# Filling products booked as two matmuls, and a norm's weights spread by products of 128 rows, at the start of a decoder trunk

## The chip, the cores and the metric

The kernel runs on one core of a Trainium2 chip. Its engines are PE (matrix products, with PEld loading the stationary operand), ACT (activations), DVE (vector work), POOL and SP; SP and POOL issue the DMAs. The metric is the device time of one execution in microseconds (us); lower is better.

## The reference, cut to what matters

Two layers over 256 tokens of width 1024. Each adds a mixer and a feed-forward part to `h`, both behind an RMS norm; a last norm gives the output.

```python
def rmsnorm(x, w):
    xf = x.astype(jnp.float32)
    y = xf * lax.rsqrt(jnp.mean(xf * xf, axis=-1, keepdims=True) + EPS)
    return (y * w.astype(jnp.float32)).astype(x.dtype)
...
    h = x
    for l in range(DEPTH):
        h = h + hybrid_mixer(rmsnorm(h, norm_mix_w[l]), w_in[l], ...)
        h = h + swiglu(rmsnorm(h, norm_ffn_w[l]), w_gate_up[l], w_down[l])
    return rmsnorm(h, final_norm_w)
```

The mixer begins with `u = h @ w_in`; its columns for the values `v` are the first that the kernel computes. All that follows here is the first norm, `rmsnorm(x, norm_mix_w[0])`, and those first products.

## The kernel before

Tokens are handled in two tiles of 128 (t = 0 and 1), the width in two halves of 512. A weight matrix comes in pieces of up to 128 x 1024 by DMA from SP (`raw`, line 309, four buffers). ACT rounds each to its high part `wh` (line 324), DVE subtracts to get the low part `wl` (line 331), and a raw buffer is free again when its `wl` is done. Each product is made of three on PE: high by high (line 340), high by low (341) and low by high (342). There are six pairs of `wh` and `wl`. The first job is `v`, in eight pieces of 128 x 512; the second is a job of 352 columns, in four pieces of 128 x 704.

For the first norm, x lands in `h` in four quarters. ACT squares each with a running sum (line 206), DVE adds the sums of a tile (`ms`, line 221), POOL raises them to the power -1/2 (`rstd`, line 226), and DVE forms `sil` = h times rstd times the norm's weights (line 216). The weights arrive as one row (`wb`, 1 x 1024) and are spread to all 128 partitions by two products with a row of ones (`wps`, line 1347), which stay in PSUM. Then PE transposes `sil` (`tr`, line 382; the identity is in `cst`), ACT copies the result to the high part of `xT` (line 206), and DVE forms its low part (line 213).

The order of all instructions is made ahead of time. `Flow` runs a model of the engines: every step is an `Op` with an engine, a cost in ns and a priority, and whenever an engine is free in the model, the ready step of the lowest priority number goes next in that engine's program. What the model decides is the order; the chip then works each engine's program in order, with semaphores. A cost that is too low makes the model place more steps into a gap than fit there.

`warm_pe` fills PE's gaps at the start. It issues two products of zeros of 384 columns, and then, as long as no real product has been issued, single ones of 64 columns (`idle`, line 1332) with priority 1000, so each goes where nothing else is ready in the model. A float32 product is executed as two passes, so each of these stands in the trace as two pieces. The last 128 columns of `zeros` hold, on partition 0, the ones for the spreading. `w_row` issues the w row on SP between the rows of x and the identity, and `rest_of_consts` issues the other constants (128 x 2048) behind the eight pieces of the first job.

Of the kernel before, what the change touches and what calls it, by code (L numbers as in the profile page):

```python
# [16 lines left out]
P = 128  # L17
# [164 lines left out]
def trunk_kernel(  # L182
# [5 lines left out]
    nc = tc.nc  # L188
# [11 lines left out]
    fl = Flow()  # L200
# [8 lines left out]
    def dve(n, pr, fn):  # L209
        return Op("dve", 1.04 * n + 69, fn, pr)  # L210
# [17 lines left out]
    def pe(cost, pr, fn):  # L228
        return Op("pe", cost, fn, pr)

    def mm_cost(n, fp32=False):
        return n * 4 / 2.4 + 4 if fp32 else max(n / 2.4 + 13.4, 110)
# [65 lines left out]
    def feeder():  # L298
        for i, (src, k, n, ev, job) in enumerate(specs):
            if i == 2:  # L300
                fl.set(first_pieces)
                yield rest_pieces
            yield rawS

            def load():
                raw = new_raw()
                dst, at = raw[:, : k * n].rearrange("p (k n) -> p k n", k=k), 0
                for part in src:
                    nc.sync.dma_start(out=dst[:, :, at : at + part.shape[2]], in_=part)
                    at += part.shape[2]  # L310
                return raw

            raw = yield Op("sp", 450, load, job)
            fl.spawn(splitter(raw, k, n, ev, job, fl.transfer(512 * k * n)))
# [982 lines left out]
    def whole():  # L1297
        norms = [Norm(norm_mix_w[0]), Norm(norm_mix_w[1]), Final(final_norm_w)]
        zeros = new_sx("zeros")
        yield sxS  # L1300
        junk = cp.tile([P, 2], F32, tag="junk", name="junk")

        def fills():
            nc.vector.memset(mhalf, -0.5)
            nc.vector.memset(zeros[:, : 3 * P], 0.0)
            nc.vector.memset(zeros[:1, 3 * P :], 1.0)

        def load(dst, src):
            return Op("sp", 450, lambda: nc.sync.dma_start(out=dst, in_=src), -1)

        def x_half(t, n):
            nsl = slice(n * 512, (n + 1) * 512)
            yield load(h[t][:, nsl], x[0, t * P : (t + 1) * P, nsl])
            fl.spawn(arrived(t, n, fl.transfer(4 * P * 512)))

        def arrived(t, n, ns):
            yield ns
            yield from norms[0].half(t, n, -1)

        def warm():  # L1320
            yield Op("act", 1400, lambda: nc.scalar.activation(out=junk, in_=mhalf, func=AF.Copy), -2)

        def warm_pe():

            yield accS
            box = []

            def emit(n, times):
                if not box:
                    box.append(new_acc("idle"))  # L1330
                for _ in range(times):
                    nc.tensor.matmul(box[0][:, :n], lhsT=zeros[:, :P], rhs=zeros[:, :n], start=True, stop=True)  # L1332

            yield pe(WARM * 1700, -2, lambda: emit(3 * P, WARM))
            while not started[0]:
                yield pe(mm_cost(64, True), 1000, lambda: emit(64, 1))
            fl.release(accS)
            fl.release(sxS)

        def spread_w(n):  # L1340

            yield smS
            nsl = slice(n * 512, (n + 1) * 512)

            def emit():
                ps = new_sm("wps")
                nc.tensor.matmul(ps, lhsT=zeros[:1, 3 * P :], rhs=first_w[:1, nsl], start=True, stop=True)
                return ps

            ps = yield pe(mm_cost(512, True), -1, emit)  # L1350
            fl.set(norms[0].wb[n], ps)

        def w_row():
            yield load(first_w[:1, :], norm_mix_w[0].rearrange("(o d) -> o d", o=1))
            fl.spawn(w_arrived(fl.transfer(4 * D)))

        def w_arrived(ns):
            yield ns
            for n in range(2):
                yield from spread_w(n)  # L1360

        def w_free():
            fl.release(wbS)
            for _ in range(2):
                fl.release(smS)

        yield wbS
        first_w = new_wb()
        norms[0].free = w_free
        yield dve(8, -2, fills)  # L1370
        fl.spawn(warm())
        fl.spawn(warm_pe())
        yield from x_half(0, 0)
        yield from x_half(0, 1)
        yield from w_row()
        yield load(ident, consts[:, K_ID : K_ID + P])
        fl.transfer(4 * P * P)
        fl.spawn(feeder())
        yield first_pieces
        yield from x_half(1, 0)  # L1380
        yield from x_half(1, 1)
        fl.set(rest_pieces)
        fl.spawn(rest_of_consts())
        for l in range(DEPTH):
            yield from layer(l, norms[l], norms[l + 1])

    def rest_of_consts():
        yield 9000.0
        yield Op("sp", 450, lambda: nc.sync.dma_start(out=cst[:, K_ID + P :], in_=consts[:, K_ID + P :]), -1)

    with tc.manual_schedule():
        fl.spawn(whole())
        fl.run()
# [50 lines left out]
```

## Time and profile before

| | us |
|---|---|
| median of 3 runs (lowest, highest) | 1300.35 (1299.91, 1300.78) |
| the profiled execution | 1293.97 |
| its span | 1292.2 |
| PE, DVE, ACT, POOL busy in it | 1282.0, 860.5, 739.6, 34.2 |

The profile is of one execution. A row of the trace names an engine, a line of the kernel, the operation and its tiles (out<-in), the count of instructions merged into it, and what ended the engine's idle time ahead of it, if there was any. Busy times of PE overlap from one product to the next, so the distance of two starts says more than a duration.

### The profile page before, as it was taken

To read this page: it belongs to the slowest core of one execution; us is meant where nothing else is said; L and a number is where in the kernel's file an instruction comes from. 1 tells how busy PE (TensorE), PEld (TensorE's weight loads), DVE (VectorE), ACT (ScalarE), POOL (GpSimd) and SP (SyncE) were. 2 spreads that over 40 slices of the span, in tenths; PEclk is the share of its full clock that TensorE was granted. 3 is DMA by queue.
4 is the path that set the end of the run, shared out by engine and by line. 5 is a ranking of instruction groups with operands and counts; after the bars stand their busy time and mean duration, and the time that the engine had idled before them with its cause. 6 is when DMAs were issued, how large, how long until landed. Compare 5 with 4: busy or idle time off the path is not lost.

```text
span 1292.2 us, 17009 instructions
## 1 busy us (share of the span) xinstructions
PE 1282.0 (99%) x6346; PEld 1078.7 (83%) x6346; DVE 860.5 (67%) x1163; ACT 739.6 (57%) x1086; POOL 34.2 (3%) x56
## 2 busy tenths in 40 slices
PE   9999999999999999999999999999999999999997
PEld 7888888888888888888888988888888888788886
DVE  5875788878576665554478658878875756655544
ACT  5765676886365454444367556867955634544432
POOL 1000000000010000000010000000000100000000
PEclk9999999999999999999999999999999999999999
DMA  7757565555465556665566565656555664766551
GB/s 225 230 164 223 163 183 164 177 195 196 147 226 198 166 192 197 183 194 189 162 190 197 165 199 161 187 181 181 196 168 179 199 209 131 233 190 189 188 188 57
DMA packets 129013, 237.67 MB, mean 184 GB/s; under 512 B 7817, under 2 KB 59905, under 8 KB 128802
## 3 DMA queue, kind: packets, MB, share of 16 engines
q1 hardware_dynamic: 127458, 232.16, 57.9%
q0 software_dynamic: 1472, 4.42, 1.2%
q8 instruction: 50, 0.82, 0.3%
q14 instruction: 33, 0.27, 0.1%
HBM read 235.43 MB, written 1.11 MB: 183 GB/s over the span
## 4 chain that ended last, share of the span: by engine, by line
PE 94%; issue 2%; DMA 1%; ACT 1%; DVE 1%; POOL 0%; POOLq 0%; SPq 0%; DVEq 0%; ACTq 0%
PE acc L340 22%; PE acc L342 22%; PE acc L341 22%; PE acc L521 10%; PE acc L522 6%; PE tr L382 3%; PE yps L1060 2%; PE acc L524 1%; DMA raw<-in_w_gate_up_dram 1%; PE idle L1332 1%; PE tr L954 1%; PE sm L819 1%; DVE wl L331 1%; PE ips L1047 0%; ACT wh L324 0%
## 5 line engine op out<-in xcount | busy, mean ns | idle before, releaser
L331 DVE TENSOR_TENSOR wl<-raw,wh 128x1024 fp32r<-128x1024 f32 (+2 forms) x432 | 514.4, 1195 | 306.4 <-ACT wh L324 304.1
L324 ACT ACTIVATE wh<-raw 128x1024 fp32r<-128x1024 f32 (+2 forms) x432 | 443.6, 1035 | 354.7 <-PE acc L342 275.8
L340 PE MATMUL acc<-wh,xT 128*128 128x512 f32 (+1 forms) x896 | 348.3, 389 | 0.0
L341 PE MATMUL acc<-wl,xT 128*128 128x512 f32 (+1 forms) x896 | 342.7, 383 | 0.2 <-DVE wl L331 0.2
L342 PE MATMUL acc<-wh,xT 128*128 128x512 f32 (+1 forms) x896 | 342.8, 383 | 0.0
L521 PE MATMUL acc<-xT,wh 128*128 128x512 f32 x560 | 203.6, 401 | 0.0
L342 PEld LDWEIGHTS acc<-wh,xT 128*128 128x128 f32 x896 | 168.2, 188 | 31.9
L341 PEld LDWEIGHTS acc<-wl,xT 128*128 128x128 f32 x896 | 168.4, 188 | 31.2 <-DVE wl L331 1.1
L340 PEld LDWEIGHTS acc<-wh,xT 128*128 128x128 f32 x896 | 168.3, 188 | 30.2 <-issue 0.9
L522 PE MATMUL acc<-xT,wl 128*128 128x256 f32 x640 | 167.0, 281 | 0.0
L522 PEld LDWEIGHTS acc<-xT,wl 128*128 128x128 f32 x640 | 120.8, 189 | 6.9
L521 PEld LDWEIGHTS acc<-xT,wh 128*128 128x128 f32 x560 | 105.4, 188 | 21.3
L340 PE MATMUL acc<-wh,A 128*128 128x512 f32 x192 | 76.7, 399 | 0.0
L216 DVE SCALAR_TENSOR_TENSOR cb<-ca,cv,cb 128x255 f32<-128x255 f32 (+1 forms) x144 | 68.4, 479 | 10.9 <-ACT cb L206 9.8
L342 PE MATMUL acc<-wh,A 128*128 128x512 f32 x192 | 74.8, 390 | 0.0
L341 PE MATMUL acc<-wl,A 128*128 128x512 f32 x192 | 74.8, 389 | 0.0
L340 PE MATMUL acc<-wh,Y 128*128 128x512 f32 x176 | 70.7, 402 | 0.0
L342 PE MATMUL acc<-wh,Y 128*128 128x512 f32 x176 | 68.7, 390 | 0.0
L341 PE MATMUL acc<-wl,Y 128*128 128x512 f32 x176 | 68.5, 389 | 0.0
L340 PE MATMUL acc<-wh,C 128*128 128x512 f32 x128 | 50.6, 395 | 0.0
L342 PE MATMUL acc<-wh,C 128*128 128x512 f32 x128 | 49.9, 390 | 0.0
L341 PE MATMUL acc<-wl,C 128*128 128x512 f32 x128 | 49.8, 389 | 0.0
(140 smaller groups left out, 1301.3 us busy)
## 6 DMA issues: line engine op xcount, KB each, us to landing
raw<-in_w_in_dram SPq DMA_DIRECT2D x188, 512.0 KB, 4.3
raw<-in_w_gate_up_dram SPq DMA_DIRECT2D x80, 512.0 KB, 3.8
raw<-in_w_down_dram SPq DMA_DIRECT2D x44, 512.0 KB, 3.2
raw<-in_ret_out_dram SPq DMA_DIRECT2D x32, 512.0 KB, 3.6
raw<-in_ssd_out_dram SPq DMA_DIRECT2D x32, 512.0 KB, 3.3
raw<-in_w_in_dram SPq DMA_DIRECT2D x24, 352.0 KB, 3.3
seg<-acs SPq DMA_DIRECT2D x16, 512.0 KB, 5.6
raw<-in_w_o_dram SPq DMA_DIRECT2D x16, 512.0 KB, 3.3
```

Source lines behind the costliest of these rows:

```text
L216: return Op("dve", 1.04 * n + 130, lambda: nc.vector.scalar_tensor_tensor(out=out, in0=in0, scalar=scalar, in1=in1, op0=op0, op1=op1), pr)
L324: nc.scalar.activation(out=wh[:, :m], in_=raw[:, :m], func=AF.Copy)
L331: nc.vector.tensor_tensor(out=wl[:, :m], in0=raw[:, :m], in1=wh[:, :m].bitcast(F32), op=ALU.subtract)
L340: nc.tensor.matmul(ps, lhsT=lh, rhs=rh, start=first, stop=False)
L341: nc.tensor.matmul(ps, lhsT=lh, rhs=rl, start=False, stop=False)
L342: nc.tensor.matmul(ps, lhsT=ll, rhs=rh, start=False, stop=last)
L382: nc.tensor.transpose(out=ps[:, j * P : (j + 1) * P], in_=src[:, j * P : (j + 1) * P], identity=ident)
L521: nc.tensor.matmul(a, lhsT=wh[:, k % 4, fsl], rhs=x[:, k % 4, :, :], start=k == 0, stop=False)
L522: nc.tensor.matmul(a[:, :SEQ], lhsT=wl[:, k % 4, fsl], rhs=xh[:, k % 4, :], start=False, stop=False)
L524: nc.tensor.matmul(a, lhsT=wh[:, k % 4, fsl], rhs=x[:, k % 4, :, :], start=False, stop=True)
L819: nc.tensor.matmul(ps[:, :SEQ], lhsT=k[:, b, :P], rhs=q[:, b, :], start=b == 0, stop=b == 1)
L1060: nc.tensor.matmul(ps[:, i * HD : (i + 1) * HD], lhsT=sg[:, i, :], rhs=xdt[:, i * HD : (i + 1) * HD], start=True, stop=True)
```

## The change

Three edits at the start, in `whole`. A filling product of 64 columns is booked in the model at twice its former cost. The two spreading products take all 128 rows of `zeros` and of `first_w` in place of row 0; for that `zeros` is filled with zeros over all 512 columns, and `first_w` is filled with zeros by POOL. The w row's DMA waits for that fill (`cleared`), and `w_row` runs beside the issue of the identity and no longer ahead of it.

```diff
             nc.vector.memset(mhalf, -0.5)
-            nc.vector.memset(zeros[:, : 3 * P], 0.0)
+            nc.vector.memset(zeros, 0.0)
             nc.vector.memset(zeros[:1, 3 * P :], 1.0)
...
             while not started[0]:
-                yield pe(mm_cost(64, True), 1000, lambda: emit(64, 1))
+                yield pe(2 * mm_cost(64, True), 1000, lambda: emit(64, 1))
...
-                nc.tensor.matmul(ps, lhsT=zeros[:1, 3 * P :], rhs=first_w[:1, nsl], start=True, stop=True)
+                nc.tensor.matmul(ps, lhsT=zeros[:, 3 * P :], rhs=first_w[:, nsl], start=True, stop=True)
...
         def w_row():
+            yield cleared
             yield load(first_w[:1, :], norm_mix_w[0].rearrange("(o d) -> o d", o=1))
...
         yield dve(8, -2, fills)
+        cleared = Event()
+
+        def clear():
+            yield Op("pool", 1000, lambda: nc.gpsimd.memset(first_w, 0.0), -2)
+            fl.set(cleared)
+
+        fl.spawn(clear())
         fl.spawn(warm())
         fl.spawn(warm_pe())
         yield from x_half(0, 0)
         yield from x_half(0, 1)
-        yield from w_row()
+        fl.spawn(w_row())
         yield load(ident, consts[:, K_ID : K_ID + P])
```

On PE, from the first instruction to the first products of the job (`acc`), the fillings between the steps of the norm change their number:

```order
 L1332 MATMUL idle<-zeros 128x384 x2
 L1332 MATMUL idle<-zeros 128x64 x2
 L1347 MATMUL wps<-wb,zeros 128x512 x2
-L1332 MATMUL idle<-zeros 128x64 x7
+L1332 MATMUL idle<-zeros 128x64 x3
 L382 MATMUL tr<-cst,sil 128x128 x4
-L1332 MATMUL idle<-zeros 128x64 x2
+L1332 MATMUL idle<-zeros 128x64
 L382 MATMUL tr<-cst,sil 128x128 x4
-L1332 MATMUL idle<-zeros 128x64 x12
+L1332 MATMUL idle<-zeros 128x64 x6
 L340 MATMUL acc<-wh,xT 128x512
```

Eleven of the 64-column fillings are gone: four ahead of the first transposes, one between them and the second, six ahead of the first real products. The steps of the norm and the products keep their order.

On SP, at the start, the identity (`cst`, 128 x 128) and the w row (`wb`) change places:

```order
 L1309 DMA h_81<-in_x_dram 128x512 x2
+L1309 DMA cst<-consts_dram 128x128
 L1309 DMA wb<-in_norm_mix_w_dram 1x1024
-L1309 DMA cst<-consts_dram 128x128
 L309 DMA raw<-in_w_in_dram 128x512 x2
 L1309 DMA h_82<-in_x_dram 128x512 x2
 L309 DMA raw<-in_w_in_dram 128x512 x6
```

The w row now waits for POOL's fill, and behind it stand the first two weight pieces, the rows of x of the second tile and the other six pieces of the first job. On POOL that fill stands ahead of everything else that the kernel itself asks for. ACT keeps its order, and so does DVE.

## Rows read from the trace of the kernel before

**Rows 1.** The page: busy time, share of the span and instructions of each engine.

```profile
PE 1282.0 (99%) x6346; PEld 1078.7 (83%) x6346; DVE 860.5 (67%) x1163; ACT 739.6 (57%) x1086; POOL 34.2 (3%) x56
```

**Rows 2.** The waits of PE from 20 us to the end: engine, line and tile that waited, what it waited for, us in total, times, longest.

```profile
PE tr L382 <- DVE sil L213: 0.9, 2, 0.5
PE tr L382 <- DVE sil L216: 0.5, 2, 0.3
PE yps L1060 <- ACT seg L1028: 0.4, 1, 0.4
```

**Rows 3.** The timeline of PE, up to the first products of the second job (352 columns): start and duration in us, line, tiles, count.

```profile
4.81 1.98 PE L1347 MATMUL wps<-wb,zeros 1*128 1x512 f32 x4
6.72 2.12 PE L1332 MATMUL idle<-zeros 128*128 128x64 f32 x14
8.63 1.06 PE L382 MATMUL tr<-cst,sil 128*128 128x128 f32 x4
9.49 0.95 PE L1332 MATMUL idle<-zeros 128*128 128x64 f32 x4
10.23 1.06 PE L382 MATMUL tr<-cst,sil 128*128 128x128 f32 x4
11.09 2.94 PE L1332 MATMUL idle<-zeros 128*128 128x64 f32 x24
13.84 0.48 PE L340 MATMUL acc<-wh,xT 128*128 128x512 f32 x1
...
15.48 1.05 PE L382 MATMUL tr<-cst,sil 128*128 128x128 f32 x8
16.28 0.47 PE L340 MATMUL acc<-wh,xT 128*128 128x512 f32 x1
...
19.30 0.49 PE L341 MATMUL acc<-wl,xT 128*128 128x512 f32 x1 [0.23 <-DVE wl L331]
...
27.00 0.32 PE L341 MATMUL acc<-wl,xT 128*128 128x352 f32 x1
```

**Rows 4.** The timeline of ACT: squares of x (sil<-h), copies of the transposes (xT<-tr), and the high part of the first 704-column piece.

```profile
7.71 0.63 ACT L206 ACTIVATE sil<-h 128x512 f32<-128x512 f32 x1 [0.40 <-DMA h<-in_x_dram]
...
9.73 0.60 ACT L206 ACTIVATE xT<-tr 128x512 fp32r<-128x512 f32 x1 [1.29 <-PE tr L382]
10.22 0.62 ACT L206 ACTIVATE sil<-h 128x512 f32<-128x512 f32 x1
...
11.33 0.60 ACT L206 ACTIVATE xT<-tr 128x512 fp32r<-128x512 f32 x1 [0.39 <-PE tr L382]
...
24.95 0.79 ACT L324 ACTIVATE wh<-raw 128x704 fp32r<-128x704 f32 x1 [2.86 <-DMA raw<-in_w_in_dram]
```

**Rows 5.** The timeline of DVE: the fill of zeros, the normed rows, the low halves of xT and of the weight pieces.

```profile
0.93 0.38 DVE L1305 MEMSET zeros<- 128x384 f32 x1
...
6.03 1.54 DVE L216 SCALAR_TENSOR_TENSOR sil<-h,rstd,wps 128x512 f32<-128x512 f32 x2 [0.95 <-PE wps L1347]
...
10.36 0.69 DVE L213 TENSOR_TENSOR xT<-tr,xT 128x512 fp32r<-128x512 f32 x1 [1.59 <-ACT xT L206]
...
11.96 0.69 DVE L213 TENSOR_TENSOR xT<-tr,xT 128x512 fp32r<-128x512 f32 x1 [0.78 <-ACT xT L206]
12.57 1.40 DVE L216 SCALAR_TENSOR_TENSOR sil<-h,rstd,wps 128x512 f32<-128x512 f32 x2
13.88 1.29 DVE L331 TENSOR_TENSOR wl<-raw,wh 128x512 fp32r<-128x512 f32 x2
...
25.77 0.89 DVE L331 TENSOR_TENSOR wl<-raw,wh 128x704 fp32r<-128x704 f32 x1 [2.96 <-ACT wh L324]
```

**Rows 6.** Busy time of each engine by stretch: the stretch in us, its length, busy us and instructions of each engine, the granted clock of PE as a share of full speed, the DMA share, GB/s.

```profile
7.50:8.00 0.50, 0.50 (x7) 0.50 (x6) 0.50 (x2) 0.28 (x1) 0.00 (x0) 0.99 0.75 279
8.00:8.50 0.50, 0.50 (x5) 0.50 (x5) 0.50 (x2) 0.44 (x2) 0.00 (x0) 0.50 1.00 381
...
11.00:11.50 0.50, 0.50 (x5) 0.50 (x4) 0.18 (x2) 0.17 (x1) 0.24 (x1) 0.60 0.13 45
...
12.00:14.00 2.00, 2.00 (x20) 2.00 (x19) 2.00 (x4) 1.48 (x3) 2.00 (x4) 1.00 0.14 31
```

**Rows 7.** The timeline of POOL: the last of four one-column fills that stand ahead of the kernel's own work, and the power of the first tile's norm.

```profile
0.33 0.12 POOL L1430 MEMSET const-uint8-127<- 128x1 uint8 x1
5.16 0.55 POOL L226 TENSOR_TENSOR rstd<-ms,mhalf 128x1 f32<-128x1 f32 x1 [4.71 <-DVE ms L221]
```

**Rows 8.** The timeline of SP's queue: when it issued which DMA.

```profile
0.74 0.87 SPq L1309 DMA_DIRECT2D h<-in_x_dram  x2
1.66 0.33 SPq L1309 DMA_DIRECT2D wb<-in_norm_mix_w_dram  x1
2.03 0.35 SPq L1309 DMA_DIRECT2D cst<-consts_dram  x1
...
3.37 0.91 SPq L1309 DMA_DIRECT2D h<-in_x_dram  x2
...
15.58 0.42 SPq L1389 DMA_DIRECT2D cst<-consts_dram  x1
```

**Rows 9.** Time from issue to landing: first of the four quarters of x, then of the two blocks of constants (the identity is the lowest, the megabyte the highest).

```profile
DMA to landing us min/median/max: 2.7/3.6/5.0
DMA to landing us min/median/max: 3.2/5.4/7.5
```

## The prediction

> **What bounds the kernel now.** I read the page first: PE is busy for 1282.0 us, 99% of the span [rows 1]. The waits of PE from 20 us to the end then show what is left to gain after the start: 1.8 us in five waits [rows 2]. So after 20 us PE sets the time, and what moves its work by a microsecond at 20 us moves the end by a microsecond, unless some transfer does not move along. The whole change lies ahead of 20 us, so I read that stretch engine by engine.
>
> PE looks full there, but most of it is filling [rows 3]. Real products begin only at 13.84. What stands before them is the first norm: the products that spread its weights (wps) at 4.81, the normed rows (sil) on DVE from 6.03, four transposes at 8.63 and four at 10.23, their copies (xT) on ACT at 9.73 and 11.33 [rows 4], and the same for the second 128 tokens, whose eight transposes start at 15.48. The reader should see three things. The first sil was finished at about 6.8 (two in 1.54 us from 6.03 [rows 5]), but its transposes start at 8.63: 14 filling pieces from 6.72 on stand ahead of them. The 24 pieces from 11.09 to 13.84 hold back products whose first operands were there by 11.05 (10.36 plus 0.69, the low half of xT [rows 5]). [...] The four transposes at 8.63 take 0.86 us to the next row, the eight at 15.48 take 0.80: 0.215 against 0.10 each. [...]
>
> Each filling is two pieces. At full clock 24 pieces take 2.75 us [rows 3], 0.115 each, 0.23 a filling; the planner before books 0.11. That is why its fillings overrun, and the new price of 0.22 is about right.
>
> **The change, part by part.**
>
> *Larger zero fill.* DVE's row is 0.38 us for 384 columns [rows 5], 1.0 ns each; 128 more cost 0.13 us. PE is busy from its first filling on, so wps moves from 4.81 to 4.94. It is on the path, but has cover: see the point on the seven fillings.
>
> *POOL's fill, and the w row behind it.* No row shows a POOL fill of 1024 columns. Below: 0.12 us, its one-column fill [rows 7], if width cost nothing. Nearest: DVE's rate, 1.0 us. Above: three times that, 3.0. I take 1.0, because both engines' small fills are of one size (0.12 here). POOL starts when all engines do, about 0.74, SP's first issue [rows 8], so the fill ends near 1.75. SP now issues the identity at 1.66 and the w row at 2.03, and waits for the fill ahead of the latter: at 1.0 it does not wait. All that is queued behind on SP (two weight pieces, the second tokens' rows of x, six pieces) would slip by any such wait, at 3.0 us by 1.7.
>
> *The w row is 0.37 us later.* It was there by 4.81, at most 3.15 after its issue; the identity, issued in the slot it gets now, took 3.2 [rows 9]. So it lands by about 5.2, and wps starts between 4.94 and 5.2. Rows 128 deep cost no more: a transpose does 128 columns in 0.10, so 512 take 0.40, and a wps piece takes 0.48 (four from 4.81 to 6.72). The first sil followed 1.22 behind wps (6.03 less 4.81); it then starts at 6.16 to 6.45 and ends at 6.9 to 7.2.
>
> *Seven fillings become three.* wps and its tail take 1.91 (6.72 less 4.81), so fillings start at 6.85 to 7.1 and six pieces of 0.115 end at 7.5 to 7.8. The transposes start there, not at 8.63. At full clock they take 0.40, and with the 0.24 from the next row to ACT's copy (9.73 less 9.49) xT could start at 8.2 to 8.4. Now ACT is late instead: its square of the second tokens starts at 7.71, because their rows of x land then, and ends after 0.63, and the read of its sum follows [rows 4]. So the copy goes from 9.73 to about 8.5, 1.25 sooner. The next square needs x's last quarter: the longest landing is 5.0 us [rows 9], from an issue near 3.83 [rows 8], so 8.85; it starts at 8.95 in place of 10.22. The second copy follows 0.7 later, at 9.7 in place of 11.33, since its transposes (one filling, 0.23, behind the first ones) are done by 9.0.
>
> On DVE the low half of that copy goes from 11.96 to 10.3, the second tokens' sil from 12.57 to 11.05, and the split low halves (wl) queued behind it from 13.88 to about 12.4: 1.45 sooner. If the clock fell as before, transposes at 0.215 and fillings at 0.185 (four from 9.49 to 10.23) would put the first copy at 8.95, the second at 10.2 and wl at 12.8: 1.1 sooner.
>
> *Twelve fillings become six.* They end near 10.3, the six products of some 1.5 us (13.84 to 15.48, less one filling) near 11.8, and the transposes of the second tokens wait for DVE (11.05 plus two of 0.7) and end near 12.9, in place of 16.28. DVE then runs its four steps of some 0.6 to the last low half of the first job back to back from 13.7: the product that waited for that one moves from 19.30 to 16.3. PE is **3.0 us** ahead here.
>
> *What is late next.* PE cannot keep that. SP issues the big block of constants at 15.58, behind two pieces that waited for the wl of 13.88; it moves by 1.45 only. The first 704-column piece lies behind that megabyte, which takes 7.5 us to landing [rows 9]; ACT waited 2.86 us for it, until 24.95 [rows 4], and DVE's low half of it ended at 25.77 plus 0.89, 26.66 [rows 5]. PE took it at 27.00 [rows 3], 0.3 later. So it is ready 1.45 sooner, at 25.2, where PE would want it at 24.0: a new wait of 1.2 us. The gain is 0.3 and 1.45, less some 0.15 because the pieces meet POOL's small transfers longer: **1.6 us**. The pieces after it are issued as buffers come free and move along.
>
> **The sum.** The profiled execution took 1293.97 us; less 1.6 gives 1292.4. The runs' median is 1300.35, 6.4 above the profiled one; the start is the same work in both, so I take the difference over: **1298.75**.
>
> [...] In the stretch from 8.0 on PE did eight transposes and fillings, and the clock rose after it [rows 3, 6]. [...]
>
> **The rivals.**
>
> *Full gain.* The piece behind the constants comes sooner than I think, because the DMA share was 0.14 at 12 to 14 us [rows 6] and there is room. Then PE keeps 2.75 to 3.0: 1297.5. Against it: 2.86 us of waiting for exactly that transfer.
>
> *The clock falls on real products.* PE now waits near 11.8 and for four wl between 13 and 16.3. At half clock a group of three products takes 1.4 in place of 0.7. A stretch as long as from 8.0 to 11.4 costs 1.7, of which 1.2 is hidden in the new wait: gain 1.1, 1299.2. Two such stretches cost 3.4, and the time is 1300.95.
>
> *POOL's fill is slow, and SP waits.* This one ends on the other side. Each microsecond over 1.3 in the fill goes to SP, to x's rows and to all pieces behind. At 3.0 us nothing is left of the gain; at 6.0 the start is 3.0 later than now: 1303.4. For it: SP works in order, and POOL takes 0.55 for one column of the power at 5.16 [rows 7]. Against: its plain fill of one column takes 0.12.
>
> *The fillings hide nothing.* x's landings hold ACT at 7.71 anyway, and the w row or POOL's first power comes late; 0.3 to 0.9 is left: 1299.8.
>
> **How the numbers follow.** Forecast 0.56 (1298.3 to 1299.2); full gain 0.14; clock 0.08; slow fill 0.07, most of it between no gain and 2 us lost; fillings hide nothing 0.15. The range is 1297.3 to 1300.6: it takes in full gain, one slow stretch and the last case, and leaves out the slow fill, two slow stretches and the tails. A measurement of this kernel can tell about 0.2%, 2.6 us, from no change. Faster than 1297.75 needs nearly the full gain: 0.11. Slower than 1302.95 is the far end of the slow fill, or several slow stretches: 0.04. Between: 0.85.
>
> **What would show it.** POOL's fill of wb near 1.0 us, and no gap on SP ahead of the w row. Six pieces ahead of the first transposes, which start near 7.6 at a granted clock of 1.00. ACT's first copy at 8.5, DVE's third low half near 12.4, the product that waited at 19.30 near 16.3; and then, as the test of the size, a wait of PE near 24 to 25 us for the first 704-column piece. If PE runs through there, the gain is 2.7 or more; if the fill lasts over 3 us, the forecast's sign is wrong.

## The result, and the profile after

The change takes 1291.86 us, median of 4 runs (1291.36 to 1292.69), against 1300.13 for the kernel before in the same comparison: a ratio of 0.9937, interval 0.992 to 0.9954. That is 8.3 us, five times the 1.6 that was forecast, and below the range. The profiled executions tell another story: 1293.97 before and 1291.82 after, 2.15 apart, close to the forecast. So two things have to be explained: the start as the profiles show it, and 6 us that the profiled execution of the kernel before does not have and its other runs do. One execution of all that follow, of e11, took 1836.11 us at a mean granted clock of 0.658 and is left out of every figure below.

First the profile after, in the views that answer to those of before. The timeline of PE, to be read beside [rows 3]:

```profile
4.96 2.71 PE L1347 MATMUL wps<-wb,zeros 128*128 128x512 f32 x4
7.50 0.78 PE L1332 MATMUL idle<-zeros 128*128 128x64 f32 x6
8.12 0.61 PE L382 MATMUL tr<-cst,sil 128*128 128x128 f32 x4
8.56 0.33 PE L1332 MATMUL idle<-zeros 128*128 128x64 f32 x2
8.73 0.61 PE L382 MATMUL tr<-cst,sil 128*128 128x128 f32 x4
9.17 1.45 PE L1332 MATMUL idle<-zeros 128*128 128x64 f32 x12
10.43 0.48 PE L340 MATMUL acc<-wh,xT 128*128 128x512 f32 x1
...
12.08 1.25 PE L382 MATMUL tr<-cst,sil 128*128 128x128 f32 x8
13.08 0.48 PE L340 MATMUL acc<-wh,xT 128*128 128x512 f32 x1
...
16.21 0.50 PE L341 MATMUL acc<-wl,xT 128*128 128x512 f32 x1 [0.23 <-DVE wl L331]
...
24.38 0.42 PE L340 MATMUL acc<-wh,xT 128*128 128x352 f32 x1 [0.47 <-ACT wh L324]
25.31 0.43 PE L341 MATMUL acc<-wl,xT 128*128 128x352 f32 x1 [0.50 <-DVE wl L331]
```

Real products start at 10.43 in place of 13.84, and the product that waited for the last low half of the first job runs at 16.21 in place of 19.30. At 24.38 and 25.31 PE waits for the first 704-column piece, as it did not before. ACT and DVE, beside [rows 4, 5]:

```profile
8.84 0.58 ACT L206 ACTIVATE xT<-tr 128x512 fp32r<-128x512 f32 x1
...
9.93 0.58 ACT L206 ACTIVATE xT<-tr 128x512 fp32r<-128x512 f32 x1
...
23.54 0.79 ACT L324 ACTIVATE wh<-raw 128x704 fp32r<-128x704 f32 x1 [4.02 <-DMA raw<-in_w_in_dram]
```

```profile
0.95 0.48 DVE L1305 MEMSET zeros<- 128x512 f32 x1
...
6.92 1.54 DVE L216 SCALAR_TENSOR_TENSOR sil<-h,rstd,wps 128x512 f32<-128x512 f32 x2 [1.81 <-PE wps L1347]
...
11.15 1.40 DVE L216 SCALAR_TENSOR_TENSOR sil<-h,rstd,wps 128x512 f32<-128x512 f32 x2
12.47 1.29 DVE L331 TENSOR_TENSOR wl<-raw,wh 128x512 fp32r<-128x512 f32 x2
```

The new fill on POOL, and SP's issues, beside [rows 7, 8]:

```profile
0.74 0.95 POOL L1375 MEMSET wb<- 128x1024 f32 x1 [0.29 <-POOLq L1438]
```

```profile
2.13 0.33 SPq L1309 DMA_DIRECT2D wb<-in_norm_mix_w_dram  x1
...
14.16 0.42 SPq L1397 DMA_DIRECT2D cst<-consts_dram  x1
```

The fill ends at 1.69 and SP issues the w row without a wait. The one thing that looks worse than forecast is the first sil, at 6.92: the four spreading pieces start 0.96, 0.73 and 0.43 apart, so the clock rose only while they ran.

### The profile page after: what moved, and what is told of

The parts are those of the page before. It is cut to its first block, busy times and chain, and to the rows that moved or that the text cites. A ratio compares the mean times of both kernels' runs of the same rounds, so it can differ in the third digit from the quotient of the medians.

```text
span 1290.1 us, 16966 instructions
## 1 busy us (share of the span) xinstructions
PE 1279.6 (99%) x6324; PEld 1075.5 (83%) x6324; DVE 860.5 (67%) x1163; ACT 739.4 (57%) x1086; POOL 35.1 (3%) x57
## 4 chain that ended last, share of the span: by engine, by line
PE 87%; DVE 4%; ACT 3%; issue 3%; DMA 3%; POOL 0%; SPq 0%; POOLq 0%; DVEq 0%; ACTq 0%
PE acc L340 21%; PE acc L342 21%; PE acc L341 21%; PE acc L521 9%; PE acc L522 5%; PE tr L382 2%; PE yps L1060 2%; DVE wl L331 2%; DMA raw<-in_w_in_dram 1%; PE acc L524 1%; ACT wh L324 1%; ACT seg L1028 1%; PE sm L819 1%; DMA seg<-acs 1%; PE tr L954 0%
```

## The experiments

The kernel before ran 78 times beside the experiments: 50 runs lie at 1299.0 or above (the late group below), 19 at 1295.5 or below (the early group), 9 between. Its time is therefore two groups with a few runs in the middle, and a kernel is best read by where its runs lie, not by its median alone. The late share differs, 18 of the 35 runs beside e1 to e4 and 32 of the 43 beside the others, so the ratios of those two parts of the table can't be set against each other. The table counts all fillings of a kernel, with the one behind the first six products.

| kernel | spreading rows | fillings of 64 columns | runs: lowest, median, highest | ratio to before (interval) |
|---|---|---|---|---|
| e1, before again | 1 | 24 | 1294.1, 1300.5, 1300.9 | 1.0018 (0.9999 to 1.0036) |
| e2, rows only | 128 | 24 | 1292.3, 1293.2, 1295.4 | 0.9976 (0.9961 to 0.9991) |
| e3, price only | 1 | 13 | 1291.8, 1294.7, 1296.0 | 0.9976 (0.9960 to 0.9993) |
| e4, the change with one row | 1 | 13 | 1291.6, 1293.2, 1296.1 | 0.9968 (0.9951 to 0.9984) |
| e5, the change again | 128 | 13 | 1291.7, 1292.7, 1294.9 | 0.9950 (0.9935 to 0.9966) |
| e6, before, no fillings | 1 | 0 | 1292.4, 1293.1, 1293.8 | 0.9956 (0.9938 to 0.9974) |
| e7, before, wide fillings | 1 | 13 of 256 | 1291.7, 1294.8, 1297.4 | 0.9967 (0.9951 to 0.9983) |
| e8, the change, constants later | 128 | 13 | 1291.3, 1292.4, 1294.2 | 0.9949 (0.9929 to 0.9969) |
| e9, the change, no fillings | 128 | 0 | 1291.4, 1292.8, 1295.9 | 0.9956 (0.9941 to 0.9971) |
| e10, before, half price | 1 | 47 | 1306.8, 1310.1, 1310.9 | 1.0081 (1.0057 to 1.0104) |
| e11, e2 with one row | 1 | 24 | 1293.5, 1297.2, 1300.5 | 0.9984 (0.9967 to 1.0001) |

**e1: the kernel before, once more**, unchanged.

> The unchanged kernel again, for the 6.4 us between its profiled execution (1293.97) and its other runs (1300.1). Theory clock (the one-row spreading products leave the clock low, and for longer in most executions than in the profiled one): runs near 1300 with a mean granted clock of about 0.990 to 0.994, and a profile near 1300 shows 0.50 well beyond 11.4 us. Theory elsewhere (the 6.4 us lie in some later part of the kernel): a clock of 0.997 as in the first profile, and rows that differ only after 20 us.

This time the profiled execution was one of the late group: 1299.67, span 1297.9. Its PE timeline:

```profile
4.96 3.78 PE L1347 MATMUL wps<-wb,zeros 1*128 1x512 f32 x4
8.67 3.25 PE L1332 MATMUL idle<-zeros 128*128 128x64 f32 x14
11.71 1.06 PE L382 MATMUL tr<-cst,sil 128*128 128x128 f32 x4
12.56 0.95 PE L1332 MATMUL idle<-zeros 128*128 128x64 f32 x4
13.31 1.06 PE L382 MATMUL tr<-cst,sil 128*128 128x128 f32 x4
14.16 5.22 PE L1332 MATMUL idle<-zeros 128*128 128x64 f32 x24
19.14 0.77 PE L340 MATMUL acc<-wh,xT 128*128 128x512 f32 x1
...
22.16 1.68 PE L382 MATMUL tr<-cst,sil 128*128 128x128 f32 x8
23.60 0.48 PE L340 MATMUL acc<-wh,xT 128*128 128x512 f32 x1
```

Read the distances: 14 filling pieces in 3.04 us and 24 in 4.98, 0.21 each, where the 24 of the first profile, most of them at a granted clock of 1.00 [rows 6], took 0.115 [rows 3]. Everything up to 23 us went at half clock: the products from 19.72 to 21.85 stand 0.43 apart, where those from 14.15 on in the first profile stand 0.23 apart, and the eight transposes from 22.16 on take 1.44 us, between the 1.70 of that pace (0.85 for four) and the 0.80 of the first profile [rows 3], which puts the rise at about 23.4. Real products began at 19.14, not 13.84, and those behind the second tokens' transposes at 23.60, not 16.28: 7.3 us late, of which 5.7 reached the end (1297.9 against 1292.2). The mean clock of 0.998 that I had expected lower does not show it: the view by stretches reads 1.00 in all of 2 to 29 us of this execution, with the pieces 0.21 apart. So in this execution the 6 us lie in the start and are a matter of the clock. The first profile of before was an execution in which the clock had risen at about 4.6 (PE's weight loads take 0.33 us at 4.30, 0.23 at 4.51 and 0.18 at 5.34) and was low again only from 8.0 to about 11.4 (0.50, and 0.60 at 11.0 to 11.5 [rows 6]). The other runs have no rows, but their mean clocks fit: 46 of the 50 late runs read 0.999 and the other four 0.998, as the profiled execution of e1 does, while 14 of the 19 early ones read 0.997, as the first profile of before does, and five 0.998.

**e2, e3, e4: each edit alone.**

```diff
# e2, against the change
-                yield pe(2 * mm_cost(64, True), 1000, lambda: emit(64, 1))
+                yield pe(mm_cost(64, True), 1000, lambda: emit(64, 1))
# e3, against the kernel before
-                yield pe(mm_cost(64, True), 1000, lambda: emit(64, 1))
+                yield pe(2 * mm_cost(64, True), 1000, lambda: emit(64, 1))
# e4, against the change
-                nc.tensor.matmul(ps, lhsT=zeros[:, 3 * P :], rhs=first_w[:, nsl], start=True, stop=True)
+                nc.tensor.matmul(ps, lhsT=zeros[:1, 3 * P :], rhs=first_w[:1, nsl], start=True, stop=True)
```

> The change without the new price of a filling, so with 128-row spreading products, 23 fillings in place of 12, and the w row behind POOL's fill. Theory clock: 1292.5 to 1294, most of the gain, and a clock of 0.998 or 0.999 in all runs. Theory filling (the fillings' overrun carries the gain): 1298 to 1300. Theory queue (the changed order on SP carries it): as for clock, to be told apart by the run with one row.

> The kernel before with the new price of a filling alone: one-row spreading products, 12 fillings. Theory clock: 1297 to 1300, a clock below 0.997 in its runs, a gain of 0 to 3 us. Theory filling: about 1292. Theory queue: 1298.5, the 1.6 us of the prediction.

> The change with one-row spreading products; the order on every engine, POOL's fill and the place of the w row are those of the change. Theory clock: 1297 to 1300, as with the price alone, because only the rows count. Theories filling and queue: 1291.9, as the change.

All three lie at 1293.2 to 1294.7, and no run of any is above 1296.1. That contradicts each theory as I had put it. The clock theory expected the price alone to leave most runs near 1300; the filling theory expected the rows alone to. Either edit by itself removes the late group, and by the medians the two do not add (6.5 us and 5.1 alone, 7.6 together in e5). So I formed another: a loop. At half clock the fillings take nearly twice as long (0.21 us a piece against 0.115); by the theory they do not bring the clock up, products of the job (the real products) do, and these stand behind the fillings; fewer fillings shorten the loop, spreading products of 128 rows ahead of it keep PE out of it. This is too narrow in one point: in the first profile of before the clock rose at about 11.4 [rows 6], ahead of the first real product at 13.84 [rows 3], and e7 and e11 show the same.

One pair of profiles shows what the rows alone do. e4 and e8 (below) have the same order on PE up to the real products, and in both the clock rose at about 5.0, just as the spreading began: the four spreading pieces take 1.91 us in e4 (5.07 to 6.98) and 1.86 in e8 (4.96 to 6.82), against 3.71 in e1 (4.96 to 8.67). Stretches of 3 us; the column behind the busy times is the granted clock. First e4, with one-row products:

```profile
5.00:8.00 3.00, 3.00 (x14) 1.68 (x14) 1.73 (x4) 1.39 (x3) 0.55 (x1) 1.00 0.97 309
8.00:11.00 3.00, 3.00 (x19) 3.00 (x17) 2.65 (x6) 3.00 (x8) 0.98 (x2) 0.57 0.78 268
11.00:14.00 3.00, 3.00 (x10) 2.52 (x10) 2.42 (x4) 0.76 (x2) 2.39 (x5) 0.50 0.30 50
14.00:17.00 3.00, 3.00 (x17) 2.68 (x17) 0.86 (x2) 1.49 (x3) 0.00 (x0) 0.80 0.88 110
```

Then e8, with 128-row products:

```profile
5.00:8.00 3.00, 3.00 (x17) 2.04 (x17) 1.72 (x3) 1.14 (x2) 0.55 (x1) 1.00 1.00 318
8.00:11.00 3.00, 3.00 (x24) 2.70 (x23) 2.25 (x5) 2.91 (x9) 0.64 (x2) 1.00 0.80 279
11.00:14.00 3.00, 2.48 (x16) 2.03 (x15) 3.00 (x6) 2.37 (x6) 2.74 (x5) 1.00 0.22 45
```

PE is busy for all of 5 to 11 us in both. After one-row products the clock fell at about 8.4 and stayed low until 15.2 (an estimate from the 0.57 of 8 to 11 and the 0.80 of 14 to 17, with the 0.50 and 1.00 that other stretches read); after 128-row products it stayed at 1.00, and the products from 10.07 to 11.00 stand 0.23 apart. The runs agree: eight of the twelve of e4 read a mean clock of 0.996 or 0.997, while all thirteen of the change (with e5) read 0.998 or 0.999. But these eight are the fast ones of e4, at 1291.6 to 1293.7. Its other four, at 1295.2 to 1296.1, read 0.999, as the late runs of the kernel before do.

**e5: the change again**, unchanged.

> The change once more, for how far its executions spread and for a profile in which the clock rises at another moment. Theory loop (at half clock the fillings take twice as long and do not raise the clock, so the real products, which do, come late; 128-row spreading products extend the dense start, so the clock has risen by 11 us in every execution): 1291 to 1293 in all runs, none above 1294. Theory luck (four runs that happened to start well): some runs at 1294 to 1300.

No run is in the late group. Three of nine lie above 1293, and one of them, at 1294.85, is over the bound of 1294. In its profile the spreading pieces take 2.88 us, from 5.31 to 8.19, and in the first profile of the change 2.54, from 4.96 to 7.50. Both lie between the 1.86 of e8 and the 3.71 of e1, so the clock rose during the spreading, by these distances at about 7.5 and 6.5.

**e6, e7: no fillings, and wide ones, in the kernel before.**

```diff
# e6
-            while not started[0]:
-                yield pe(mm_cost(64, True), 1000, lambda: emit(64, 1))
# e7
-                yield pe(mm_cost(64, True), 1000, lambda: emit(64, 1))
+                yield pe(mm_cost(128, True), 1000, lambda: emit(256, 1))
```

> The kernel before, with one-row spreading products, without any 64-column filling; PE idles in their place. Theory loop: no run at 1300; the real products start at 12 to 14 us at either clock, and the time is 1291.5 to 1296, as with the new price alone. Theory guard (the fillings keep the clock up, or bring it up): more runs at 1300 or above, since nothing is left between the one-row products and the real ones but transposes.

> The kernel before with fillings of 256 columns, booked at half of what they take, so that they overrun by about as much time as those of 64 columns did: 13 in place of 24, one-row spreading products. If the width of a filling decides whether it raises the clock (theory loop), the clock rises during the fillings, and the runs lie at 1292.5 to 1296 with none at 1300. If fillings only take time, whatever their width, the runs spread from 1294 to 1301 as before, most at 1300.

Without any filling the kernel before takes 1293.1 with a spread of 1.4 us: the fillings did not guard the clock, they were the delay. In its profile the clock stayed low until about 12 (the products up to 11.66 stand 0.43 to 0.49 apart, from 12.07 on 0.23), and yet the real products began at 9.72, sooner than the 12 to 14 that I had expected:

```profile
7.92 2.03 PE L382 MATMUL tr<-cst,sil 128*128 128x128 f32 x8
9.72 0.79 PE L340 MATMUL acc<-wh,xT 128*128 128x512 f32 x1
```

The wide ones of e7 overrun at least as much (3.57 us ahead of the first transposes, where e1 has 3.04), and yet no run is above 1297.4. Six of the twelve are above the 1296 that I had set, though, at 1296.2 to 1297.4. The PE timeline of one of these:

```profile
8.78 3.78 PE L1332 MATMUL idle<-zeros 128*128 128x256 f32 x8
12.35 1.06 PE L382 MATMUL tr<-cst,sil 128*128 128x128 f32 x4
13.20 0.97 PE L1332 MATMUL idle<-zeros 128*128 128x256 f32 x2
14.01 0.60 PE L382 MATMUL tr<-cst,sil 128*128 128x128 f32 x4
14.45 2.76 PE L1332 MATMUL idle<-zeros 128*128 128x256 f32 x12
16.86 0.58 PE L340 MATMUL acc<-wh,xT 128*128 128x512 f32 x1
```

Four transposes take 0.85 us at 12.35 and 0.44 at 14.01: the clock rose between them, three microseconds ahead of the first real product. With narrow fillings, in e1, it had not. Transposes stood ahead of this rise too, so the profile alone does not show that the width did it.

**e10: twice the fillings in the kernel before.**

```diff
-                yield pe(mm_cost(64, True), 1000, lambda: emit(64, 1))
+                yield pe(mm_cost(64, True) / 2, 1000, lambda: emit(64, 1))
```

> The kernel before with a filling booked at half its former price: 47 fillings where 24 stood, one-row spreading products. Theory loop: at half clock 46 more pieces of 0.213 us stand ahead of the real products, and the clock waits for those: most runs 9 to 10 us later, at 1308 to 1311. Where the clock was up early, 0.115 a piece: 1298 to 1300. If the 1300 state does not come from the fillings, most runs stay at 1300 to 1302.

All six runs are at 1306.8 to 1310.9, 9.7 us behind the kernel before at the median. Four lie where the loop puts them; the other two, at 1306.8 and 1307.0, do not reach the 1298 to 1300 that I had given for an early rise. The profile is of one of these two: the clock was up early (the spreading pieces take 1.90 us, from 5.20 to 7.10), but fell at about 7.9 (0.98 at 5 to 8, 0.50 at 8 to 11). Its PE timeline and its stretches (granted clock behind the busy times):

```profile
15.34 10.77 PE L1332 MATMUL idle<-zeros 128*128 128x64 f32 x50
25.87 0.77 PE L340 MATMUL acc<-wh,xT 128*128 128x512 f32 x1
```

```profile
17.00:20.00 3.00, 3.00 (x16) 3.00 (x15) 2.42 (x4) 0.74 (x2) 1.04 (x2) 0.50 0.38 33
20.00:23.00 3.00, 3.00 (x16) 3.00 (x15) 0.00 (x0) 0.00 (x0) 0.00 (x0) 0.50 0.80 247
23.00:26.00 3.00, 3.00 (x16) 3.00 (x15) 0.00 (x0) 0.00 (x0) 0.00 (x0) 0.50 0.68 270
```

For ten microseconds PE is busy without a gap, with nothing but 64-column fillings, at half clock. The clock rose at about 28.35 (0.61 at 26 to 29), 2.5 us after the first real product. This is the loop in one view.

**e11: e2 with one-row products.** The edit is that of e4, made in e2.

> The run with the rows alone (e2: 128 rows, old price, 23 fillings, POOL's fill, the w row behind the identity), with one-row products in place of 128-row ones; the order is that of e2 on every engine. Theory loop: most runs at 1298 to 1301, since the rows were all that e2 had against the slow state. If the order on SP or the two more fillings ahead of the spreading did it: 1292.5 to 1295.5, as e2.

Of eleven runs five are at 1300.0 or above, where e2 has none above 1295.4; that is fewer than the most that the loop gave. Three lie near 1297, three at 1293.5 to 1294.0, and the median is 1297.2. The order is that of e2 on every engine, so at the old price the rows alone are worth 4.0 us at the median. What is left of e2's gain, the 3.1 us from 1300.3 to 1297.2, is not clear of the spread (the interval of the ratio ends at 1.0001), so a smaller part for the order on SP or the fillings ahead of the spreading is not excluded. At the new price (e4 against e5) the rows are worth 0.5 at the median, and the four runs above 1295 that e4 has are missing in e5.

**e8, e9: what is left.**

```diff
# e8, against the change
-        yield 9000.0
+        yield 20000.0
# e9, against the change
-            while not started[0]:
-                yield pe(2 * mm_cost(64, True), 1000, lambda: emit(64, 1))
```

> The change with the megabyte of constants issued later, behind the four pieces of 128 x 704 and three more. It removes the wait of PE at 24 to 25 us for the first of those pieces (0.65 and 0.75 us in the profile of the change). If that wait was what took back a part of the gain, the first product of the second job starts 1.3 us sooner and the time is 0.5 to 1.3 us below the change; if the next pieces are late by as much, the same as the change.

> The change without any 64-column filling. Theory loop: the clock rises during or right behind the 128-row spreading products as in the change, and what is left of the overrun goes too: 1291 to 1292.5, a median 0 to 0.7 us below the change. Theory guard (twelve fillings keep the clock up until the real products): the clock falls in some executions, up to 1294.

Neither differs from the change by more than its runs spread, and neither forecast of a gain came true. In e8 the wait at 24 us is gone, and another one stands a job later:

```profile
23.74 0.32 PE L340 MATMUL acc<-wh,xT 128*128 128x352 f32 x1
...
38.32 0.50 PE L340 MATMUL acc<-wh,xT 128*128 128x512 f32 x1 [1.12 <-ACT D L206]
```

The first product of the second job starts 0.64 us sooner than in the profile of the change (23.74 against 24.38), where 1.3 was forecast, the second 1.41 sooner; at 38.32 only 0.4 of the lead is left (38.74 in the change).

In e9 the median, 1292.8, is no better than that of e5, and five of twelve runs lie at 1293.75 to 1295.91, where e5 has one of nine above 1293.5. Two of these five read a mean clock of 0.997, as the first profile of before, in which it fell. That is what the theory of the guard gave, so with 128-row products the twelve fillings may do some good; the runs don't settle it. No version was found that beats the change.

## Why the prediction was wrong

**The step that failed** is the sum: "the start is the same work in both, so I take the difference over". The profiled execution lay 6.4 us below a median whose three runs spread by 0.9. I took that as an offset common to both kernels. It was the very cost that the change removes: in the late executions of the kernel before the clock stays low until the real products, and the profiled one had escaped. In e1, the one late execution with a profile, the clock was low until about 23.4 us, and PE was 7.3 us late, of which 5.7 reached the end. That the other late runs are like it is argued from their times and mean clocks. What half clock costs was in the rows: fillings at 0.185 a piece there against 0.115 [rows 3, 6]. Without the offset the sum says 1292.4, and 1291.86 was measured.

**Luck.** That the two profiles differ by 2.15, close to the 1.6, is in part luck: they are of executions with different clocks. Before, the clock was up from 4.6 to 8.0 and low until about 11.4 [rows 6]; after, it was low until 6.5 and up from there. In e8, with the same order on PE and a rise at about 5.0, the real products began at 9.75 in place of 10.43.

**The larger zero fill** cost 0.10 (0.48 less 0.38), and PE's first filling moved from 1.36 to 1.49, by the 0.13 forecast. That wps started at 4.96 for 4.94 does not show it: in e1 it starts at 4.96 too, without the larger fill. **POOL's fill** took 0.95 for 1.0, with luck: I took DVE's rate for POOL's because their small fills are of one size, but DVE's fill of two columns takes 0.06 and POOL's of one 0.12. SP did not wait, the w row went out at 2.13 for 2.03 and landed in time in this profile; in that of e5 wps started at 5.31, 0.1 over my bound.

**Seven fillings to three.** They end at 8.12 for 7.5 to 7.8, because the clock rose only during the spreading, which took 2.54 in place of 1.91. ACT's copies came at 8.84 and 9.93 for 8.5 and 9.7, the second sil at 11.15 for 11.05, wl at 12.47 for 12.4. **Twelve to six.** They end at 10.43 for 10.3; the second tokens' transposes at 13.08 for 12.9; the product that waited at 16.21 for 16.3. **What is late next** was right in place and size: constants issued at 14.16 for 14.13, the piece's high part at 23.54 for 23.5, and PE took the low half at 25.31 for 25.2. The gain there is 27.00 less 25.31, 1.69 for 1.6; the 0.15 that I took off for POOL's small transfers has no row in any run. The profiles' spans end 2.1 apart, 0.4 more than that; behind 26 us PE waits 0.7 us in place of 1.8 [rows 2], which may be where it comes from.

**The rivals.** Full gain did not come, for the reason given: PE's lead of 3.09 us at 16.21 was 1.69 at 25.31. The slow fill did not happen. That the fillings hide nothing is refuted by the profile after (real products at 10.43 for 13.84), by e6 and by e10. A fall of the clock on real products did not come in the profile after: the granted clock is 1.00 throughout, and from 16.55 to 22.71 the products stand 0.22 to 0.24 apart. Three products at half clock take 1.28 us (19.72 to 21.00 in e1) against 0.70 (14.15 to 14.85 in the first profile of before), not 1.4. The clock rival looked at the wrong kernel: I asked whether the change would let the clock fall on real products, and not whether the clock was low on those of the kernel before in the runs that set its median, as it was in e1 until about 23.4. And the fall to 0.50 at 8.0 in the first profile [rows 6], behind one-row products and narrow fillings [rows 3], I took for a fact of that one execution and gave no price in the others.

## What to carry to other kernels

If a profiled execution lies outside the spread of the other runs, the profile is of another case: find what differs before taking its rows as a price for the median. A filling product that overruns its price delays the work behind it, at half clock nearly twice as much (0.21 us a piece against 0.115). None was shown to be worth its place here: without any, the kernel before took 1293.1 and the change 1292.8, no more than with them. A filling booked at what it takes at half clock, about 0.42 us, was not tried. After such an edit, read the clock from the distance of like products, and several runs instead of one.

## What the runs showed of the hardware that I had not expected

Products with one row of operands did not hold the clock, though PE was busy for as long: with them the clock fell at about 8.4 and was 0.50 at 11 to 14 (e4), with 128 rows it was 1.00 from 5 to 14 (e8). Width seems to count too: fifty 64-column pieces back to back left it at 0.50 for ten microseconds (e10), while with 256-column ones in the place of narrow ones no run of twelve was late (e7, highest 1297.4).

Transposes may bring the clock up. In e11 nothing but eight transposes and narrow fillings stood between the one-row products and the rise; PE's timeline:

```profile
11.85 1.06 PE L382 MATMUL tr<-cst,sil 128*128 128x128 f32 x4
12.70 0.95 PE L1332 MATMUL idle<-zeros 128*128 128x64 f32 x4
13.45 1.05 PE L382 MATMUL tr<-cst,sil 128*128 128x128 f32 x4
14.30 2.82 PE L1332 MATMUL idle<-zeros 128*128 128x64 f32 x24
16.93 0.48 PE L340 MATMUL acc<-wh,xT 128*128 128x512 f32 x1
```

The fillings from 14.30 on take 0.11 a piece to the product at 16.93, where the four from 12.70 on took 0.19, so the clock was up, and no real product had run. The rise at about 11.4 in the first profile of before stands behind eight transposes as well [rows 3, 6], and narrow fillings alone did not raise it in e10. In e1 the same eight transposes at 11.71 to 14.16 did not raise it (the fillings behind them take 0.21 a piece), so the moment seems to matter as well; what decides that was not tried.
